# The low part of a pair's second weight tile by a VectorE subtraction in place of an accumulating DMA

## The chip, the cores and the metric

The kernel runs on one core of a Trainium2 chip. The time is device microseconds of one execution on that core. A kernel's time is the median of several runs. One execution more is taken by the hardware profiler, and all the rows shown below come from that one. The engines are named as in the profile: PE is TensorE's matmul, PEld its weight load, DVE is VectorE, ACT is ScalarE, POOL is GpSimd, SP is SyncE.

## The reference

One layer of a hybrid decoder runs over 520 columns (512 prompt positions and 8 sample positions). The part that matters here is the channel mixer at the end of the layer, with `wg`, `wu` of 1024 x 3072 and `wd` of 3072 x 1024, all float32:

```python
def conv_ffn(xn, prefix, wg, wu, cw, cb, wd):
    g_pre = xn @ wg
    ext = jnp.concatenate([prefix.astype(g_pre.dtype), g_pre], axis=1)
    h = jax.nn.gelu(causal_dwconv(ext, cw, cb)) * (xn @ wu)
    return h @ wd, ext[:, -(FFN_CONV - 1):]
...
    f, ffn_state = conv_ffn(rmsnorm(x, lp['norm2_g']), ffn_prefix, lp['ffn_wg'], lp['ffn_wu'],
                            lp['ffn_conv_w'], lp['ffn_conv_b'], lp['ffn_wd'])
    x = x + f
```

## The kernel before, in words

**Numbers in two parts.** A float32 weight tile is used as a sum of two float32r tiles: the high part `wh` is the tile rounded by an ACT copy, the low part `wl` is the tile minus its high part. The activations are split likewise. A product is three matmuls: high by high (`wh` with `X..h`), high weight by low activation (`wh` with `X..l`), and low weight by high activation (`wl` with `X..h`), in this order for each block of 128 rows (lines 202 to 207 and 256 to 258). A weight tile here is 128 x 1024 float32, 512 KB.

**Two ways to make a low part.** `Chunk.low` (line 120) makes it with a DVE subtraction of raw and high part (line 127). `low_by_dma` (line 97) makes it in two steps: ACT writes minus the high part into the low tile (line 99), and a DMA issued by POOL adds the weights from DRAM onto it (line 100). The DMA reads the weights from DRAM a second time, so it needs no raw tile. Ten chunks of the stage before the pairs go this second way too.

**The stages.** Up to about 472 us the mixers and their projections run, then comes the first part of the channel mixer with plain tiles. From 547.70 us to 900.69 us in the trace it runs in 18 **pairs** (`MP = 6`, lines 1055 to 1058): a pair is two column blocks of 128 of `wg` or of `wu`, nine pairs of `wg` and nine of `wu`, in turns. After the last pair come the last `wd` blocks and the final norm.

**One pair.** Its two raw tiles `raw[0]` and `raw[1]` are multiplied as 2 x 2 blocks by the half-size scheme with seven products. The weight operands are `h1` (`raw[1]` itself), `h0` (half of `raw[0]`), and two sums `h2`, `h3`, built by four DVE additions (lines 176 to 181). `run_pair` (line 244) emits PE's work as eleven steps by `SEQ_PAIR = (0, (0,0), 3, 2, (0,1), 1, 4, 5, (1,0), 6, (1,1))`: a number is one of the seven products, of 12 matmuls, and a bracket is half of one of two filler jobs, 12 matmuls of the `wd` product. So a pair is 132 matmuls. Product 0 takes the first half of `h1`, and the third matmul of the pair is the first that reads the low part of `h1`. Products 2 and 3 take the first halves of `h3` and `h2`, and product 6 takes `h0`.

**What sets the order.** Each engine works through its own list in the order in which the program emits it. After every step `run_later` emits the helper steps that are due. `Pair.steps` (line 189) gives their due times in steps, counted back from the start of the pair: the loads at -15, the sums at -8, -7 and -6, `high1` at -7, `low1` at -6, `high0` at -6, `low0` at -5, the high and low parts of `h2` and `h3` from -4 to -2, and the low part of `h3` at +1. So `high1` and `low1` of a pair are emitted about the middle of the pair before it. The filler's `wd` chunk is loaded at -9 steps and split at -3 (ACT) and -2 (DVE).

**Queues and buffers.** SP issues all weight loads in order. Raw tiles live in four buffers (`RAW = 4`), so a load waits until the last reader of an earlier tile is done. The list of SP shows the second load of a pair waiting for DVE and for ACT. High and low tiles have six buffers each (`HS`, `LS`). POOL issues the accumulating DMAs: `wl<-in_wg`, `wl<-in_wu` of line 100, and `x1d<-dn` of line 1004, which adds each filler's result (copied by ACT, line 1003) onto a DRAM buffer. The results of products leave PSUM through ACT copies (line 261) and DVE subtractions (lines 967 and 986).

Of the kernel before, what the change touches and what calls it, by code (L numbers as in the profile page):

```python
# [51 lines left out]
def trunk_kernel(ctx: ExitStack, tc: tile.TileContext, t: dict, o: dict):  # L52
    nc = tc.nc
    v, s, g, te = nc.vector, nc.scalar, nc.gpsimd, nc.tensor
# [26 lines left out]
    def f(x):  # L81
        return x.bitcast(F32)
# [14 lines left out]
    def low_by_dma(l, h, src):  # L97

        s.activation(l, f(h), AF.Copy, scale=-1.0)
        nc.gpsimd.dma_start(l, src, accum_op=ALU.add)  # L100
# [32 lines left out]
    class Pair:  # L133
# [27 lines left out]
            s.activation(self.new("h1", "wh"), self.raw[1], AF.Copy)  # L161

        def low1(self):
            low_by_dma(self.new("h1", "wl"), self.W["h1", "wh"], self.src[1])

        def high0(self):
            s.activation(self.new("h0", "wh"), self.raw[0][:, 512:], AF.Copy)
# [1041 lines left out]
```

## Time and profile before

| | us |
|---|---|
| median of 3 runs | 951.67 (946.41 to 952.67) |
| the profiled execution | 943.07 |
| its span, first to last instruction | 941.1 |
| PE busy in the span | 882.6 (94%) |
| DVE busy | 575.9 (61%) |
| ACT busy | 456.8 (49%) |
| POOL busy | 134.3 (14%) |

How to read it: busy is the time in which an engine had an instruction under way, and matmuls overlap, so a busy PE is not a PE at its peak. The rows of a timeline give start, duration, engine, line and operation, and in brackets how long the engine had been idle before and what it waited for. A wait is put down to the last of the things waited for. The granted clock (PEclk) is TensorE's, 1.00 being 2.4 GHz, and it has two levels here, 2.4 and 1.2 GHz.

### The profile page before, as it was taken

The page shows a single profiled execution, that of the slowest core. Times are in us where ns is not written, and L with a number is a line of the kernel's source. Part 1 is how long each engine was busy: PE and PEld are TensorE (multiplying, and loading weights), DVE is VectorE, ACT ScalarE, POOL GpSimd, SP SyncE. Part 2 cuts the span into 40 slices and gives each one's busy share as a digit, 9 for nine tenths or more (in the row PEclk, how much of TensorE's full clock was granted, in tenths as well). Part 3 has the DMA queues.
Part 4 walks back from the last instruction along what each step waited for, and adds up shares of the span by engine and source line. Part 5 has one row for each costly group of instructions (what it writes and reads, how often), then busy time and mean ns, then how long its engine had stood idle before and what let it go on. Part 6 is the DMA issues. An engine that isn't in the chain of part 4 may idle for free.

```text
span 941.1 us, 16904 instructions
## 1 busy us (share of the span) xinstructions
PE 882.6 (94%) x7142; PEld 874.7 (93%) x7142; DVE 575.9 (61%) x906; ACT 456.8 (49%) x651; POOL 134.3 (14%) x189
## 2 busy tenths in 40 slices
PE   9999999999999999999999997898887899889894
PEld 7999999999999999999999997888887899888894
DVE  5897987888844421555577756445555545754456
ACT  7555554773433332223477654445554455544540
POOL 1403311021000001000121411111111111111120
PEclk9999999999999999999999999899999899999997
DMA  9333233223232333324397686455666556765542
GB/s 303 125 103 112 68 102 101 68 77 103 69 112 83 96 113 127 122 90 136 135 223 161 136 186 149 113 112 136 130 150 140 120 113 144 167 138 114 113 125 92
DMA packets 38859, 117.84 MB, mean 125 GB/s; under 512 B 4456, under 2 KB 7656, under 8 KB 38760
## 3 DMA queue, kind: packets, MB, share of 16 engines
q1 hardware_dynamic: 25600, 83.21, 27.1%
q0 software_dynamic: 11808, 32.12, 20.2%
q10 hardware_dynamic: 1376, 1.44, 0.4%
q8 instruction: 56, 0.92, 0.4%
q14 instruction: 19, 0.16, 0.1%
HBM read 101.57 MB, written 15.57 MB: 124 GB/s over the span
## 4 chain that ended last, share of the span: by engine, by line
PE 62%; issue 29%; POOL 3%; DMA 2%; DVE 2%; ACT 1%; SPq 0%; POOLq 0%; DVEq 0%; ACTq 0%
PE pj L206 57%; POOL x1d L1004 2%; PE pa L257 1%; PE lru L206 1%; DMA wl<-in_wu 1%; DMA wl<-in_wg 1%; POOL wl L100 1%; DVE y L1034 1%; PE c L257 1%; DMA x<-in_x 0%; PE vm L745 0%; POOL fg L961 0%; PE po L206 0%; PE pf L257 0%; DVE bc L515 0%
## 5 line engine op out<-in xcount | busy, mean ns | idle before, releaser
L127 DVE TENSOR_TENSOR wl<-raw,wh 128x1024 fp32r<-128x1024 f32 (+1 forms) x108 | 126.5, 1176 | 42.4 <-ACT wh L118 42.4
L206 PE MATMUL pj<-xn_h,wh 128*128 128x260 f32 x704 | 141.9, 283 | 0.1
L206 PE MATMUL pj<-xn_l,wh 128*128 128x260 f32 x704 | 141.4, 282 | 0.0
L206 PE MATMUL pj<-xn_h,wl 128*128 128x260 f32 x704 | 140.8, 281 | 0.0
L118 ACT ACTIVATE wh<-raw 128x1024 fp32r<-128x1024 f32 (+1 forms) x118 | 117.6, 1005 | 4.9 <-DMA raw<-in_w_in 2.8
L206 PEld LDWEIGHTS pj<-xn_l,wh 128*128 128x128 f32 x704 | 108.6, 188 | 0.0
L206 PEld LDWEIGHTS pj<-xn_h,wh 128*128 128x128 f32 x704 | 108.1, 188 | 0.3 <-ACT r L533 0.3
L206 PEld LDWEIGHTS pj<-xn_h,wl 128*128 128x128 f32 x704 | 108.2, 188 | 0.0
L206 PE MATMUL pj<-h_l,wh 128*128 128x260 f32 x384 | 84.0, 299 | 0.0
L206 PE MATMUL pj<-h_h,wh 128*128 128x260 f32 x384 | 83.7, 298 | 0.0
L206 PE MATMUL pj<-h_h,wl 128*128 128x260 f32 x384 | 83.2, 297 | 0.0
L1004 POOL DMA_DIRECT2D x1d<-dn x40 | 34.9, 874 | 310.4 <-ACT dn L1003 300.2
L257 PE MATMUL pa<-X_h,wl 128*128 128x260 f32 x72 | 24.7, 343 | 43.6 <-DMA wl<-in_wu 24.3
L206 PEld LDWEIGHTS pj<-h_l,wh 128*128 128x128 f32 x384 | 65.3, 206 | 0.0
L206 PEld LDWEIGHTS pj<-h_h,wl 128*128 128x128 f32 x384 | 64.8, 204 | 0.0
L206 PEld LDWEIGHTS pj<-h_h,wh 128*128 128x128 f32 x384 | 64.4, 203 | 0.0
L257 PEld LDWEIGHTS pa<-X_h,wl 128*128 128x128 f32 x72 | 15.7, 218 | 47.1 <-DMA wl<-in_wu 26.2
L686 ACT ACTIVATE gt<-pj 128x520 f32<-128x520 f32 x24 | 14.5, 605 | 81.3 <-PE pj L206 81.2
L967 DVE TENSOR_TENSOR fg<-pf,m 128x260 f32<-128x260 f32 x9 | 3.9, 429 | 67.3 <-ACT dn L1003 36.9
L187 DVE TENSOR_TENSOR wl<-sum,wh 128x1024 fp32r<-128x1024 f32 x36 | 43.9, 1219 | 0.9 <-ACT wh L184 0.9
L261 ACT ACTIVATE m<-pa 128x260 f32<-128x260 f32 x36 | 14.0, 388 | 62.5 <-PE pa L257 62.4
L986 DVE TENSOR_TENSOR c<-pf,m 128x260 f32<-128x260 f32 x9 | 3.9, 429 | 57.1 <-ACT dn L1003 26.3
(480 smaller groups left out, 2430.1 us busy)
## 6 DMA issues: line engine op xcount, KB each, us to landing
raw<-in_w_in SPq DMA_DIRECT2D x50, 512.0 KB, 3.5
raw<-in_wg SPq DMA_DIRECT2D x24, 512.0 KB, 4.2
raw<-in_wu SPq DMA_DIRECT2D x24, 512.0 KB, 4.7
raw<-in_wd SPq DMA_DIRECT2D x24, 512.0 KB, 8.5
x1d<-dn POOLq DMA_DIRECT2D x40, 260.0 KB, 4.9
wl<-in_wu POOLq DMA_DIRECT2D x15, 512.0 KB, 9.4
wl<-in_wg POOLq DMA_DIRECT2D x13, 512.0 KB, 9.1
raw<-in_w_pb SPq DMA_DIRECT2D x8, 512.0 KB, 3.6
```

What stands on the lines that cost most here:

```text
L100: nc.gpsimd.dma_start(l, src, accum_op=ALU.add)
L118: s.activation(self.h[:, q], self.raw[:, q], AF.Copy)
L127: v.tensor_sub(self.l[:, q], self.raw[:, q], f(self.h[:, q]))
L187: v.tensor_sub(self.new(n, "wl"), self.s[n], f(self.W[n, "wh"]))
L206: te.matmul(ps[:, h, :TH], ww, xx[h] if isinstance(xx, list) else xx[:, h * TH:(h + 1) * TH], start=first and n == 0, stop=last and n == 2)
L257: te.matmul(bank[b], ww, xx, start=seen[b] + j + e == 0, stop=i >= (6, 1, 5)[b] and j == 3 and e == 2, skip_group_check=True)
L261: s.activation(kept["AFC"[b] + str(seen[b])], bank[b], AF.Copy)
L686: s.activation(two(y), acc(ps), AF.Sigmoid)
L967: v.tensor_sub(o_, a, b)
L986: v.tensor_sub(o_, a, b)
L1004: nc.gpsimd.dma_start(x1d[:, j, :], y, accum_op=ALU.add)
L1034: v.scalar_tensor_tensor(y[:, j - j0, :], x1[j][:, c], pc("gf", j), ps[:, 0, :TH], op0=ALU.mult, op1=ALU.mult)
```

## The change

`Pair.low1` calls the DVE subtraction in place of `low_by_dma`. The operands are the raw tile in SBUF and the high tile. Nothing else is edited: the due time stays at -6 steps.

```diff
         def low1(self):
-            low_by_dma(self.new("h1", "wl"), self.W["h1", "wh"], self.src[1])
+            v.tensor_sub(self.new("h1", "wl"), self.raw[1], f(self.W["h1", "wh"]))
```

In the lists of the engines it moves the following, once in each of the 18 pairs. On DVE, in the middle of a pair (here the first pair, of `wg`, while the next one is made ready): the sums L176 to L181 and `low0` (L170) belong to the next pair, L967 takes the running pair's product 1 (`pf`) and product 5 (`c`) out of PSUM, L187 makes the low part of `h2`. Before:

```order
L176 TENSOR_TENSOR sum<-raw 128x512
L177 TENSOR_TENSOR sum<-sum,raw 128x512
L179 TENSOR_TENSOR sum<-raw 128x512
L181 TENSOR_TENSOR sum<-sum,raw 128x512
L967 TENSOR_TENSOR fg_7023<-pf,m 128x260
L170 TENSOR_TENSOR wlq<-raw,whq 128x512
L967 TENSOR_TENSOR fg_7023<-c,m 128x260
```

And now:

```order
L176 TENSOR_TENSOR sum<-raw 128x512
L177 TENSOR_TENSOR sum<-sum,raw 128x512
L179 TENSOR_TENSOR sum<-raw 128x512
L181 TENSOR_TENSOR sum<-sum,raw 128x512
L164 TENSOR_TENSOR wl<-raw,wh 128x1024
L967 TENSOR_TENSOR fg_7019<-pf,m 128x260
L170 TENSOR_TENSOR wlq<-raw,whq 128x512
L967 TENSOR_TENSOR fg_7019<-c,m 128x260
```

The subtraction L164 stands new between the last sum of the next pair and the step that takes product 1 out of PSUM.

On ACT, in the same place (L161 is `high1` of the next pair, L167 its `high0`, L1003 copies the filler's result, L261 copies results of products). Before:

```order
L261 ACTIVATE m<-pa 128x260
L161 ACTIVATE wh<-raw 128x1024
L1003 ACTIVATE dn_6803<-pj 128x520
L99 ACTIVATE wl<-wh 128x1024
L167 ACTIVATE whq<-raw 128x512
L261 ACTIVATE k<-pa 128x260
```

And now:

```order
L261 ACTIVATE m<-pa 128x260
L161 ACTIVATE wh<-raw 128x1024
L1003 ACTIVATE dn_6801<-pj 128x520
L167 ACTIVATE whq<-raw 128x512
L261 ACTIVATE k<-pa 128x260
```

The negated copy L99 is gone, and what stood behind it moves up. On POOL the 18 issues of L100 go in the same way, and its x1d issues (L1004) then stand in a row. On PE the list of matmuls is the same in both. On SP the loads stand as before, but the second load of a pair, which waited for DVE and ACT, now waits for DVE alone.

## Rows read from the trace of the kernel before

**Rows 1.** Busy time by stretch; columns: stretch, its length, then busy us (and instructions) of PE, PEld, DVE, ACT and POOL, the granted clock, the share of the DMA engines and GB/s. The first stretch lies far ahead of the pairs, the second is all 18 pairs, then the first, the second, a later pair of `wg` and the `wu` pair after it.

```profile
236.30:471.70 235.40, 235.40 (x1970) 235.40 (x1969) 111.80 (x140) 80.69 (x103) 10.60 (x19) 1.00 0.34 109
547.70:900.69 352.99, 309.43 (x2380) 305.91 (x2379) 188.28 (x310) 179.15 (x275) 49.58 (x75) 0.94 0.61 133
547.70:563.53 15.83, 15.83 (x135) 15.83 (x134) 7.85 (x14) 9.88 (x15) 2.75 (x5) 1.00 0.73 134
563.53:582.18 18.65, 15.59 (x130) 15.39 (x129) 10.59 (x19) 9.85 (x16) 2.61 (x3) 1.00 0.61 133
704.69:724.93 20.24, 17.66 (x135) 17.45 (x134) 10.35 (x17) 10.40 (x16) 2.75 (x5) 0.92 0.59 124
724.93:745.50 20.57, 17.60 (x134) 17.39 (x133) 11.06 (x20) 9.86 (x16) 2.61 (x3) 0.92 0.59 128
```

**Rows 2.** The waits of PE from 560 to 930 us: engine, what waited, for what, us in total, times, longest.

```profile
PE pa L257 <- DMA wl<-in_wu: 24.3, 9, 3.8
PE pa L257 <- DMA wl<-in_wg: 19.3, 8, 2.7
PE n31p L452 <- DVE x2q L1019: 0.5, 1, 0.5
PE n30b L480 <- DVE n30d L459: 0.5, 1, 0.5
```

**Rows 3.** The timeline of PE at the start of a later pair of `wg`: its first three matmuls, and matmuls of fillers and products behind them.

```profile
704.69 0.29 PE L257 MATMUL pa<-X_h,wh 128*128 128x260 f32 x1
704.81 0.28 PE L257 MATMUL pa<-X_l,wh 128*128 128x260 f32 x1
707.67 0.39 PE L257 MATMUL pa<-X_h,wl 128*128 128x260 f32 x1 [2.58 <-DMA wl<-in_wg]
...
709.75 0.64 PE L206 MATMUL pj<-h_h,wl 128*128 128x260 f32 x2
...
714.85 0.40 PE L206 MATMUL pj<-h_h,wh 128*128 128x260 f32 x2
```

**Rows 4.** The timelines of ACT and POOL ahead of that pair: `high1`, the filler's copy, the negated copy, and the issue of its low part's DMA behind that of x1d.

```profile
695.10 1.05 ACT L161 ACTIVATE wh<-raw 128x1024 fp32r<-128x1024 f32 x1
696.23 0.61 ACT L1003 ACTIVATE dn<-pj 128x520 f32<-128x520 f32 x1
696.73 1.05 ACT L99 ACTIVATE wl<-wh 128x1024 fp32r<-128x1024 f32 x1
...
697.13 0.86 POOL L1004 DMA_DIRECT2D x1d<-dn  x1 [10.09 <-ACT dn L1003]
698.08 0.88 POOL L100 DMA_DIRECT2D wl<-in_wg  x1
```

**Rows 5.** The DMA issues from 560 to 900 us: what, queue, count, KB each, median us from issue to landing.

```profile
wl<-in_wg POOLq DMA_DIRECT2D x8, 512.0 KB, 9.5
wl<-in_wu POOLq DMA_DIRECT2D x8, 512.0 KB, 9.6
```

**Rows 6.** The DVE groups of all 18 pairs (547.7 to 900.7 us): line, operation, shapes, count, busy us, mean ns of one, idle time ahead of them and what ended it.

```profile
L127 DVE TENSOR_TENSOR wl<-raw,wh 128x1024 fp32r<-128x1024 f32 x19 | 23.2, 1220 | 7.0 <-ACT wh L118 7.0
...
L967 DVE TENSOR_TENSOR fg<-pf,m 128x260 f32<-128x260 f32 x9 | 3.9, 429 | 67.3 <-ACT dn L1003 36.9 <-PE pf L257 30.4
...
L986 DVE TENSOR_TENSOR c<-pf,m 128x260 f32<-128x260 f32 x9 | 3.9, 429 | 57.1 <-ACT dn L1003 26.3 <-PE pf L257 23.1 <-ACT wl L99 7.7
```

**Rows 7.** The first pair, which had no wait, and the head of the second: timeline of DVE.

```profile
549.69 0.69 DVE L181 TENSOR_TENSOR sum<-sum,raw 128x512 f32<-128x512 f32 x1
556.63 0.43 DVE L967 TENSOR_TENSOR fg<-pf,m 128x260 f32<-128x260 f32 x1 [6.25 <-PE pf L257]
557.19 0.69 DVE L170 TENSOR_TENSOR wlq<-raw,whq 128x512 fp32r<-128x512 f32 x1
559.41 0.43 DVE L967 TENSOR_TENSOR fg<-c,m 128x260 f32<-128x260 f32 x1 [1.52 <-PE c L257]
...
565.68 1.22 DVE L187 TENSOR_TENSOR wl<-sum,wh 128x1024 fp32r<-128x1024 f32 x1
566.82 0.69 DVE L176 TENSOR_TENSOR sum<-raw 128x512 f32<-128x512 f32 x1
...
568.75 0.68 DVE L181 TENSOR_TENSOR sum<-sum,raw 128x512 f32<-128x512 f32 x1
```

**Rows 8.** The same stretch on ACT, PE and SP: `high1` of the second pair and the copies around it; where the first pair's product 2 begins and where it first uses a low part; the two loads of the third pair (one row for both, the second issued at the end of the row's time), and a load of a `wd` chunk, which shows how long one issue takes.

```profile
553.94 1.05 ACT L161 ACTIVATE wh<-raw 128x1024 fp32r<-128x1024 f32 x1
...
565.80 0.64 ACT L855 ACTIVATE fc<-fc 128x520 f32<-128x520 f32 x1 [0.54 <-DVE fc L846]
568.49 0.39 ACT L261 ACTIVATE m<-pa 128x260 f32<-128x260 f32 x1 [2.05 <-PE pa L257]
...
552.02 0.28 PE L257 MATMUL pa<-X20h,wh 128*128 128x260 f32 x1
...
552.26 0.28 PE L257 MATMUL pa<-X20h,wl 128*128 128x260 f32 x1
...
545.16 10.18 SPq L153 DMA_DIRECT2D raw<-in_wg  x2
557.91 0.33 SPq L112 DMA_DIRECT2D raw<-in_wd  x1
```

**Rows 9.** Line 153 (the loads of the pairs' raw tiles): time from issue to landing, all 36.

```profile
DMA to landing us min/median/max: 3.4/4.3/6.8
```

## The prediction

> **What bounds the kernel now.** I read the busy time by stretch first, to see where PE, the engine with the most work, falls short of its own pace. Far ahead of the pairs it is busy without a gap at a granted clock of 1.00. The 18 pairs take 352.99 us, PE is busy for 309.43 of them, and the clock is 0.94 [rows 1]. The first pair is a measure of what a pair costs when nothing is late: 15.83 us, all busy, clock 1.00. The two later pairs shown take 20.24 and 20.57 us at 0.92 [rows 1]. So 18 undisturbed pairs would be 18 x 15.83 = 284.94 us, and the stage loses 352.99 - 284.94 = 68.05 us.
>
> The list of waits names the first part of the loss: PE waits 9 times for `wl<-in_wu` and 8 times for `wl<-in_wg`, 24.3 + 19.3 = 43.6 us, that is in 17 of 18 pairs, and the next entry is 0.5 us [rows 2]. The timeline shows the place: the first two matmuls of the pair run, the third, the first to read the low part of `h1`, comes 2.58 us late [rows 3]. The second part is the clock: behind the wait two filler matmuls take 0.64 us, later 0.40 [rows 3]. Over the stage it is 309.43 - 284.94 = 24.5 us of busy time too much, 1.44 us for each of 17 waits.
>
> Why it is late: `high1` starts at 695.10, the filler's copy and the negated copy follow, the x1d issue stands ahead on POOL, so that the DMA is issued at 698.08 [rows 4] and takes 9.5 us to land [rows 5]: 707.6, and PE goes on at 707.67 [rows 3].
>
> **The change part by part.**
>
> *Removed.* 18 negated copies on ACT (1.05 us each, [rows 4]), 18 issues on POOL (0.88 us) and 18 DMAs of 512 KB. ACT and POOL aren't waited for at that place, so their gain by itself is nothing. The DMA is what PE waits for, 43.6 us.
>
> *Added.* 18 subtractions on DVE. The same operation on the same shape is L127, 1.22 us [rows 6], 22 us in all. What hides them is DVE's idle time just behind them: before it takes product 1 out of PSUM, DVE idles 67.3 us in the nine `wg` pairs and 57.1 in the nine `wu` pairs [rows 6]. That idle time shrinks when the pairs do, so I look at the first pair, which already runs at the new pace: DVE idles 6.25 us up to 556.63 [rows 7]. The subtraction needs `high1`, which ends at 553.94 + 1.05 = 554.99 [rows 8]. It would run from 555.0 to 556.2 and leave DVE free 0.4 us before product 1 is there. Its result is wanted at 563.53 + 2 x 0.12 = 563.77, by the third matmul of the second pair ([rows 3] for the step of 0.12), so the low part is 7.5 us early instead of about 3 late. Were the cover gone, the price would be at most 18 x 1.22 = 22 us.
>
> *The new wait.* In DVE's list the subtraction waits for ACT's `high1`, and behind it stand the step that frees product 1's bank, `low0`, and the rest of the pair's chain. In the first pair `low0` starts at 557.19, after that step [rows 7], so with 0.4 us to spare nothing moves. The order behind product 5 (559.41 in [rows 7]) is the same as now.
>
> *What is late next.* The low part of `h3` is made last. In the first pair it ends at 565.68 + 1.22 = 566.90 [rows 7]. Product 2 reads its low part first at 552.26 - 547.70 = 4.56 us after a pair's start [rows 8], so an unstalled second pair wants it at 563.53 + 4.56 = 568.09: 1.2 us spare. On ACT the copy of product 0's result, which frees the bank for product 2, stands behind a gelu that starts at 565.80 [rows 8]. It would end at 565.80 + 0.64 + 0.39 = 566.83, against 563.53 + (552.02 - 547.70) = 567.85 for product 2's first matmul: 1.0 us spare. Both distances are set by product 5 of the pair before, not by the stall, so they hold in each pair.
>
> *The moved load.* The second raw tile is now also read by the subtraction, so the load that takes its place goes out about 1.2 us later. In the first pair it went at 545.16 + 10.18 - 0.33 = 555.0, the end of `high1` [rows 8]; now it is 556.2. The longest landing was 6.8 us [rows 9]: 563.0, and the first sum wants it at 566.82 [rows 7]. 3.8 us spare, so nothing. With the 18 x 512 KB of the accumulating DMAs gone, I expect loads no slower than now.
>
> *The clock.* The rows show 1.00 wherever PE runs without a gap, over 235 us, and in the first pair, and 0.92 where there is a wait [rows 1]. The second pair waited 3.06 us by its busy time (18.65 - 15.59) and kept 1.00 [rows 1], so not each wait costs clock, but none is lost without one. I take the whole 24.5 us as gained; the low end of this term is 0, if the clock falls for another reason. The Trainium skill, page "TensorE: Matmul & The Clock Gate", section "HAM oscillation — how this bites in real kernels", says that a loop of matmuls with a DMA wait in each round is throttled again at the waits and pays half rate each time. By that rule all of the 24.5 us goes and the profiled time is 875.0; with a clock that falls for other reasons it would be 899.5. The trace agrees with the rule in most pairs and not in the second.
>
> *The sum.* Against the profiled execution's 943.07 us (span 941.1): 43.6 for the waits and 24.5 for the clock, 0 for all else, is 68.05 (or 68.1 with the rounded terms): 943.07 - 68.05 = 875.0. This execution is 8.6 us below the median of the runs, 951.67, and below all three. If the 8.6 us lies in waits and clock, it goes too: 875.0. If it lies elsewhere, it stays: 883.6. No row decides this, so I take the middle, 879.
>
> **The rivals.**
>
> *A, part of the loss stays.* Either the clock term stays (943.07 - 43.6 = 899.5), or a small wait for `h3`'s low part or its bank takes the old wait's place. A wait of 1 us with the old clock loss in 17 pairs would be 17 x (1 + 1.44) = 41 us, so 916. For it: the spare time is only 1.0 to 1.2 us, in all pairs. Against it: the first pair ran at full pace with the same chain, and the added instruction doesn't stand in it. By the runs' median this is 890 to 925.
>
> *B, no change.* Something else is late at the same place and was hidden behind the DMA, so the edit moves the name of the wait and not its length: about 952. Against it: the operands of product 0 are the activations of before, the high part is ready at 695.10 + 1.05 = 696.15 [rows 4], and the `wd` parts have a filler's distance. Nothing in the rows holds PE at that place but the DMA.
>
> *C, slower: a loop through the raw tile.* The subtraction now holds `raw[1]`, the load of the next but one pair waits for it, the four sums wait for the load, and the next subtraction stands behind the sums in DVE's list. One turn of that loop is the landing time L, the sums from 566.82 to 569.43 (2.6 us, [rows 7]) and the subtraction's 1.22: L + 3.8 us a pair. It binds once L is over 12.0 us (15.83 - 3.8), and the kernel is slower than before once L + 3.8 is over the present mean, 352.99 / 18 = 19.6, so from L = 15.8 us. At L = 18 it would be 18 x 2.2 = 40 us more, 983 (992 by the median). Against it: these loads land in 3.4 to 6.8 us [rows 9], and the traffic falls. Even an accumulating DMA took only 9.5 [rows 5].
>
> **How the numbers follow.** Forecast 0.85, A 0.10, B 0.03, C 0.02. The predicted time is the forecast's, 879. Its own range: downward 875.0 less the spread of the three runs (952.67 - 946.41 = 6.3), 868.7; upward 883.6 and half a microsecond lost in each of 18 pairs (9.0), 892.6. So 868 to 893, which leaves 0.15 out and needs no part of A. A measurement of this kernel can tell about 1% from no change. Forecast and A are both over 1% faster: 0.95. Same 0.03, slower 0.02.
>
> **What would show it.** PE's waits in the pairs are no longer for a DMA of `wl`, and sum to a few us at most. Each pair takes about 15.8 us at a clock of 1.00, the stage about 285. DVE's new row L164 takes 1.22 us, starts right behind `high1`, and ends before DVE takes out product 1. ACT and POOL have 18 instructions fewer, and loads land within 7 us. I would be wrong if the pairs still show a granted clock near 0.92 without a wait (then A's clock), if PE waits at product 2 (A's other half), if the third matmul still waits, for DVE (B), or if the sums wait for the raw tile (C).

## The result, and the profile after

| | us |
|---|---|
| before, median of 4 runs | 949.04 (943.73 to 952.67) |
| after, median of 4 runs | 875.05 (874.69 to 875.17) |
| ratio, 95% interval | 0.9224 (0.9173 to 0.9275) |
| the profiled executions, before and after | 943.07 and 874.69 |
| their spans | 941.1 and 872.8 |

The kernel is 7.8% faster. The predicted time was 879 in a range of 868 to 893. The sum against the profiled execution gave 875.0.

The busy time by stretch, as in [rows 1], in the profile after: all 18 pairs, the first pair, and the second.

```profile
547.34:832.31 284.97, 284.97 (x2380) 284.97 (x2379) 207.64 (x327) 162.15 (x258) 34.54 (x58) 1.00 0.56 134
547.34:563.16 15.82, 15.82 (x134) 15.82 (x133) 8.97 (x15) 8.93 (x14) 1.87 (x4) 1.00 0.58 125
563.16:578.98 15.82, 15.82 (x134) 15.82 (x133) 12.21 (x21) 8.82 (x15) 1.73 (x2) 1.00 0.56 135
```

The stage takes 284.97 us, where the prediction had 18 x 15.83 = 284.94. PE is busy for all of it at a granted clock of 1.00. Before it took 352.99 us, so 68.0 us of the 68.4 us between the two profiled executions come from here.

The waits of PE, of the whole span after:

```profile
PE n31p L452 <- DVE x2q L1017: 3.3, 1, 3.3
PE warm L1084 <- DVE wz L1081: 1.5, 1, 1.5
PE n31b L480 <- POOL n31d L459: 1.4, 1, 1.4
PE n31p L452 <- DVE x2q L1019: 0.5, 1, 0.5
PE n30b L480 <- DVE n30d L459: 0.5, 1, 0.5
PE n31b L480 <- DVE n31d L459: 0.3, 1, 0.3
PE pj L206 <- ACT wh L118: 0.3, 1, 0.3
```

The two DMA entries of [rows 2], 43.6 us, are gone, and nothing has come in their place within the pairs: what is left belongs to the start and to the final norm.

The DVE groups of the pairs after, to be read against [rows 6]:

```profile
L164 DVE TENSOR_TENSOR wl<-raw,wh 128x1024 fp32r<-128x1024 f32 x17 | 20.8, 1226 | 31.8 <-ACT wh L161 31.8
L967 DVE TENSOR_TENSOR fg<-pf,m 128x260 f32<-128x260 f32 x9 | 3.9, 429 | 2.5 <-PE pf L257 2.5
L986 DVE TENSOR_TENSOR c<-pf,m 128x260 f32<-128x260 f32 x9 | 3.9, 429 | 3.9 <-PE pf L257 3.9
```

The idle time ahead of product 1's removal, 124 us before, now is 31.8 us ahead of the subtraction, which waits for `high1`, and 2.5 + 3.9 us behind it. The rest is gone because the pairs are shorter.

The first pair after and the head of the second, timeline of DVE, and rows of ACT, PE and SP:

```profile
554.66 1.23 DVE L164 TENSOR_TENSOR wl<-raw,wh 128x1024 fp32r<-128x1024 f32 x1 [4.65 <-ACT wh L161]
556.24 0.43 DVE L967 TENSOR_TENSOR fg<-pf,m 128x260 f32<-128x260 f32 x1 [0.35 <-PE pf L257]
...
565.33 1.22 DVE L187 TENSOR_TENSOR wl<-sum,wh 128x1024 fp32r<-128x1024 f32 x1
566.46 0.69 DVE L176 TENSOR_TENSOR sum<-raw 128x512 f32<-128x512 f32 x1
...
565.99 0.37 ACT L261 ACTIVATE m<-pa 128x260 f32<-128x260 f32 x1
...
567.48 0.28 PE L257 MATMUL pa<-X20h,wh 128*128 128x260 f32 x1
...
567.72 0.28 PE L257 MATMUL pa<-X20h,wl 128*128 128x260 f32 x1
...
555.92 0.33 SPq L153 DMA_DIRECT2D raw<-in_wg  x1
```

This is [rows 7, 8] shifted by about 0.36 us with the subtraction put in: it leaves DVE free 0.35 us before product 1 is there, the low part of `h3` is ready at 566.55, 1.17 us before product 2 reads it, the copy that frees product 2's bank ends at 566.36, 1.12 us before product 2's first matmul, and the load goes out as the subtraction ends. These loads land in 3.3 to 6.0 us, median 3.9, against [rows 9].

### The profile page after: what moved, and what is told of

Same layout as the page of the kernel before. It is cut to its first block, busy times and chain, and to the rows that moved or that the text cites. A ratio compares the mean times of both kernels' runs of the same rounds, so it can differ in the third digit from the quotient of the medians.

```text
span 872.8 us, 16856 instructions
## 1 busy us (share of the span) xinstructions
PE 858.1 (98%) x7142; PEld 853.9 (98%) x7142; DVE 596.1 (68%) x924; ACT 438.9 (50%) x633; POOL 119.4 (14%) x171
## 3 DMA queue, kind: packets, MB, share of 16 engines
q10 hardware_dynamic: 1376, 1.44, 0.5%
## 4 chain that ended last, share of the span: by engine, by line
PE 97%; DVE 2%; ACT 0%; DMA 0%; issue 0%; DVEq 0%; ACTq 0%
PE pj L206 73%; PE pa L257 12%; PE c L257 6%; PE pf L257 3%; PE lru L206 1%; DVE y L1034 1%; PE vm L745 0%; DMA par<-in_par 0%; PE po L206 0%; DVE bc L515 0%; PE vt L738 0%; ACT L533 0%; DVE n L468 0%; PE n31p L452 0%; PE n30p L452 0%
## 5 line engine op out<-in xcount | busy, mean ns | idle before, releaser
L206 PE MATMUL pj<-h_l,wh 128*128 128x260 f32 x384 | 78.6, 282 | 0.0
L206 PE MATMUL pj<-h_h,wh 128*128 128x260 f32 x384 | 78.6, 283 | 0.0
L1004 POOL DMA_DIRECT2D x1d<-dn x40 | 34.9, 874 | 266.0 <-ACT dn L1003 259.6
L206 PEld LDWEIGHTS pj<-h_l,wh 128*128 128x128 f32 x384 | 59.7, 188 | 0.0
L206 PEld LDWEIGHTS pj<-h_h,wl 128*128 128x128 f32 x384 | 59.7, 188 | 0.0
L206 PEld LDWEIGHTS pj<-h_h,wh 128*128 128x128 f32 x384 | 59.6, 188 | 0.0
L187 DVE TENSOR_TENSOR wl<-sum,wh 128x1024 fp32r<-128x1024 f32 x36 | 43.9, 1220 | 0.9 <-ACT wh L184 0.9
L164 DVE TENSOR_TENSOR wl<-raw,wh 128x1024 fp32r<-128x1024 f32 x18 | 22.1, 1226 | 31.8 <-ACT wh L161 31.8
L184 ACT ACTIVATE wh<-sum 128x1024 fp32r<-128x1024 f32 x36 | 37.8, 1050 | 0.8 <-DVE sum L179 0.8
L844 DVE SCALAR_TENSOR_TENSOR fc<-fg,par,fc 128x512 f32<-128x512 f32 x48 | 36.0, 750 | 1.1 <-ACT fc L840 0.3
L951 ACT ACTIVATE h_h<-fc 128x520 fp32r<-128x520 f32 x24 | 15.4, 640 | 25.4 <-DVE fc L983 11.1
L1003 ACT ACTIVATE dn<-pj 128x520 f32<-128x520 f32 x40 | 23.9, 598 | 6.6 <-PE pj L206 5.0
```

The source lines that it names most:

```text
L164: v.tensor_sub(self.new("h1", "wl"), self.raw[1], f(self.W["h1", "wh"]))
L184: s.activation(self.new(n, "wh"), self.s[n], AF.Copy)
L187: v.tensor_sub(self.new(n, "wl"), self.s[n], f(self.W[n, "wh"]))
L206: te.matmul(ps[:, h, :TH], ww, xx[h] if isinstance(xx, list) else xx[:, h * TH:(h + 1) * TH], start=first and n == 0, stop=last and n == 2)
L844: v.scalar_tensor_tensor(y[:, :SEQ], ext[:, r:r + SEQ], pc("fcw", r * MF + m), y[:, :SEQ], op0=ALU.mult, op1=ALU.add)
L951: after(0.25, lambda: s.activation(h, y, AF.Copy))
```

## The experiments

The question was what the 68 us had been paid for. Theory 1: for lateness alone, a part that PE wants about 2.6 us before it is there, plus the clock that the wait costs. Theory 2: for the accumulating DMA itself, its second reading of 9.4 MB, its POOL issues and ACT copies. Theory 3 was rival A of the prediction: that the clock has other reasons. Two more questions were how much room there is on DVE, and what bounds the kernel now.

**The DMA kept, but issued earlier** (e1 and e10, from the kernel before):

```diff
-            return ((-15, self.load), (-8, lambda: self.sums(0)), (-7, lambda: self.sums(1)), (-7, self.high1),
-                    (-6, lambda: self.sums(2)), (-6, self.low1), (-6, self.high0), (-5, self.low0),
+            return ((-15, self.load), (-8, lambda: self.sums(0)), (-7, lambda: self.sums(1)), (-10, self.high1),
+                    (-6, lambda: self.sums(2)), (-10, self.low1), (-6, self.high0), (-5, self.low0),
```

and with -8 for both in e10 (one step sooner than before for `high1`, two for `low1`).

> The accumulating DMA stays, but the high part of h1 and its negated copy are emitted 10 steps ahead of the pair instead of 7 and 6, right behind the copy of product 0's result. Theory (the wait is lateness alone, issue plus 9.5 us of landing): the copy ends about 5.2 us into the pair before, the DMA is issued at about 5.2 to 6.1 us and lands at about 14.7 to 15.6, against 16.1 when PE wants it; the 43.6 us of waits and the 24.5 us of clock go nearly all, 875 to 890 us. Rival (the DMAs cost by their 9.4 MB of traffic, their POOL issues or ACT copies, wherever they stand): the time stays over 910 us.

> The kernel before with the high part of h1 and its negated copy 8 steps ahead of the pair (before: 7 and 6; the early DMA: 10). Theory (lateness alone): the DMA is issued about 7.0 us into the pair before, 2 us earlier than in the kernel before, and PE wants it at 16.1 us; with a landing of 7.4 to 9.5 us it is late by 0 to 0.5 us: 875 to 888 us. Rival (the DMA costs its full wait at any place but the earliest): over 915 us.

Measured: 874.98 us for e1, ratio 0.9248 (0.9208 to 0.9287), and 875.55 us for e10, ratio 0.9252 (0.9225 to 0.9278). PE has no wait for `wl` in either. The timeline of POOL in e1, where the second pair starts about 563.3:

```profile
565.34 0.86 POOL L1004 DMA_DIRECT2D x1d<-dn  x1 [8.57 <-ACT dn L1003]
568.83 0.88 POOL L100 DMA_DIRECT2D wl<-in_wg  x1 [2.63 <-ACT k L261]
571.58 0.86 POOL L1004 DMA_DIRECT2D x1d<-dn  x1 [1.87 <-ACT dn L1003]
```

and the issues of e1 from 547 to 832 us, as in [rows 5]:

```profile
wl<-in_wu POOLq DMA_DIRECT2D x9, 512.0 KB, 5.7
wl<-in_wg POOLq DMA_DIRECT2D x8, 512.0 KB, 7.4
```

All 18 DMAs, negated copies and issues are still there, and the time is that of the kernel after. So the DMA costs nothing by itself here. Theory 2 falls, and two steps of due time are worth as much as the whole change.

The earlier issue did not act alone. The issue of the second pair's DMA before, where the first pair starts at 547.70, then in e10, where it starts at 547.89, and the issues of e10 from 547 to 832 us:

```profile
556.93 0.88 POOL L100 DMA_DIRECT2D wl<-in_wu  x1
...
555.13 0.89 POOL L100 DMA_DIRECT2D wl<-in_wu  x1 [5.22 <-ACT m L261]
...
wl<-in_wu POOLq DMA_DIRECT2D x9, 512.0 KB, 6.4
wl<-in_wg POOLq DMA_DIRECT2D x8, 512.0 KB, 6.7
```

The DMA goes out 2.0 us sooner in the pair, and it also lands about 3 us faster than the 9.5 of [rows 5]. So what PE waited for is the moment of landing, and the due time moved both terms of it, the issue and the landing time.

**The low part made late by DVE** (e2, from the kernel after):

```diff
+        def touch1(self):
+            l = self.W["h1", "wl"]
+            v.tensor_scalar(l, f(l), 1.0, None, op0=ALU.mult)
...
-                    (1, lambda: self.low("h3")))
+                    (0, self.touch1), (1, lambda: self.low("h3")))
```

> The kernel after, with one operation more: at the pair's start DVE multiplies the low part of h1 by 1.0 in place, so that it is ready as late as the DMA made it, but by DVE. Theory (lateness is all, whoever causes it, and the clock falls with the wait): DVE comes to it about 2 us into the pair, in both kinds of pair, it takes 0.6 to 1.2 us, PE waits 2.3 to 3.0 us in 17 pairs, 39 to 51 us, and 15 to 25 us of clock come with it: 930 to 950 us. Rival 1 (the clock falls for another reason than the wait): 915 to 925 us with a granted clock that stays at 0.99. Rival 2 (the DMA itself is the cost): under 885 us.

Measured: 922.06 us, ratio 0.9744 (0.9701 to 0.9786), 47.0 us over the kernel after. That is 8 us under the range expected: PE waits 30.9 us in 17 pairs, since in `wg` pairs DVE comes to the operation 0.7 us into the pair (583.12, the pair starting at 582.39), not 2 as I had reckoned, and the wait is 1.07 us, not 2.3 or more. By its time alone e2 lies in the range of rival 1, but that rival wanted a clock that stays at 0.99. The stage of the 18 pairs in e2, with the granted clock at 0.96:

```profile
547.98:879.12 331.14, 300.23 (x2379) 296.71 (x2378) 216.93 (x344) 163.18 (x258) 35.13 (x58) 0.96 0.47 115
```

PE is busy for 300.23 us of it, 15.3 more than in the kernel after. About 0.25 us for each of the 17 waits, 4.3 us, is lost at full clock too (the same in e5, where the clock stayed up); the other 11 us are the clock. The timeline of PE of e2, a wait that lost no clock:

```profile
566.70 0.39 PE L261 MATMUL pa<-X_h,wl 128*128 128x260 f32 x1 [2.50 <-DVE wl L168]
568.01 0.40 PE L210 MATMUL pj<-h_h,wh 128*128 128x260 f32 x2
```

and one of the same length that did:

```profile
602.43 0.39 PE L261 MATMUL pa<-X_h,wl 128*128 128x260 f32 x1 [2.48 <-DVE wl L168]
604.00 0.64 PE L210 MATMUL pj<-h_h,wh 128*128 128x260 f32 x2
...
606.17 0.64 PE L210 MATMUL pj<-h_h,wl 128*128 128x260 f32 x2
```

With no DMA in it the same kind of wait brings the same kind of loss: both parts belong to lateness, whoever is late. Theory 3 falls: waits put back bring the low clock back, though not at each wait.

**Only the `wu` pairs changed** (e7, from the kernel before; `sub` is true for `wu`, and the lines that hand it to the pair are left out here):

```diff
         def low1(self):
-            low_by_dma(self.new("h1", "wl"), self.W["h1", "wh"], self.src[1])
+            if self.sub:
+                v.tensor_sub(self.new("h1", "wl"), self.raw[1], f(self.W["h1", "wh"]))
+            else:
+                low_by_dma(self.new("h1", "wl"), self.W["h1", "wh"], self.src[1])
```

> The subtraction only in the nine wu pairs; the nine wg pairs keep the accumulating DMA. Theory (each pair's gain is its own wait and clock): what is left are the eight waits for wl of wg, 19.3 us, and 8 x 1.44 = 11.5 us of clock, so 875 + 31 = 906 us, between 900 and 912. Rival (what is removed in one pair comes back in the next): 925 to 945 us.

Measured: 906.29 us, ratio 0.9579 (0.9537 to 0.9621). The waits of PE:

```profile
PE pa L260 <- DMA wl<-in_wg: 21.8, 8, 4.0
```

21.8 us of waits and 9.4 us more make the 31.2 us over the kernel after. The gain is a sum over pairs: next to nothing removed in one pair comes back in the next, though the eight waits that are left come to 21.8 us where they were 19.3 before [rows 2]. The clock fell at four of the eight.

**Room on DVE** (e3: the new subtraction twice; e4 and e5: the low part of `h3` two and three times; all from the kernel after):

```diff
-            v.tensor_sub(self.new("h1", "wl"), self.raw[1], f(self.W["h1", "wh"]))
+            l = self.new("h1", "wl")
+            for _ in range(2):
+                v.tensor_sub(l, self.raw[1], f(self.W["h1", "wh"]))
```

```diff
-            v.tensor_sub(self.new(n, "wl"), self.s[n], f(self.W[n, "wh"]))
+            l = self.new(n, "wl")
+            for _ in range(2 if n == "h3" else 1):
+                v.tensor_sub(l, self.s[n], f(self.W[n, "wh"]))
```

In e5 there is a 3 in place of the 2.

> The kernel after with the new subtraction done twice in a row, 18 more DVE instructions of 1.22 us. Theory (it lies in idle time of DVE, and a delay of product 1's removal from PSUM reaches nobody): DVE takes product 1 out 0.8 us later, PE waits for nothing, 873 to 877 us. Rival (DVE has become the bound of the pair): 18 x 0.8 to 18 x 1.2 us more, 889 to 897 us.

> The kernel after with the low part of h3, the last part made for a pair, subtracted twice in a row: it is ready 1.13 us later. Theory (its spare time is 1.2 us where a wg pair goes before and 1.7 us where a wu pair does): PE waits for nothing or a few tenths in nine pairs, 873 to 879 us. Rival (there is no such spare time, DVE is at its limit): 17 x 1.1 us more, 890 us or over.

> The same with three subtractions: 2.27 us later. Theory: PE waits at product 2 for DVE, about 1.1 us in nine pairs and 0.6 us in eight, 14 to 15 us, and 0.2 to 0.5 us of slower start or clock each: 888 to 900 us. Rival (the low part of h3 is not what is late next): 873 to 879 us, as with two.

Measured: e3 874.64 us, ratio 0.9245 (0.9198 to 0.9293); e4 876.93, ratio 0.923 (0.918 to 0.9281); e5 895.53, ratio 0.9428 (0.9376 to 0.9479). In e3 the removal of product 1 is put off and PE doesn't notice, timeline of DVE:

```profile
555.06 2.48 DVE L166 TENSOR_TENSOR wl<-raw,wh 128x1024 fp32r<-128x1024 f32 x2 [4.62 <-ACT wh L161]
557.46 0.42 DVE L969 TENSOR_TENSOR fg<-pf,m 128x260 f32<-128x260 f32 x1
```

In e5 the next late part shows, in the waits of PE:

```profile
PE pa L259 <- DVE wl L189: 16.4, 17, 1.3
```

One more subtraction (1.13 us) ahead of `h3`'s low part uses up its spare time: in e4 a `wu` pair, which has a `wg` pair before it, takes about 16.06 us instead of 15.82, with no wait long enough to be listed, which makes up e4's 1.9 us. The second is paid: 1.24 us where a `wg` pair goes before and 0.67 us where a `wu` pair does. Rival A of the prediction names the right part, and what kept it away is 1.17 us in the one kind of boundary and about 1.7 us in the other.

**The other accumulating DMAs** (e6, from the kernel after): the ten plain chunks ahead of the pairs get the subtraction too.

```diff
-            job([(Chunk(src[i], KD, timed=True, by_dma=post is u2_post or m >= 2), 0, plain if m >= MN else (lambda k: xg2[k]))],
+            job([(Chunk(src[i], KD, timed=True, by_dma=False), 0, plain if m >= MN else (lambda k: xg2[k]))],
```

> The kernel after, and the ten plain chunks ahead of the pairs that take an accumulating DMA get the subtraction too, 10 x 1.22 us more on DVE, 10 DMAs, negated copies and POOL issues fewer. Theory (only a part that PE waits for is worth anything, and PE waits for none of these): 873 to 877 us. Rival (removing the DMAs is worth something by itself, as traffic or as ACT and POOL time): 865 to 872 us. Other rival (DVE is short of time in that stage, 9 tenths busy in places): 880 to 890 us.

Measured: 874.61 us, ratio 0.9206 (0.9146 to 0.9266). No difference that can be told from 875.05. The same edit, at a place where nobody waits for the part, is worth nothing.

**Earlier loads** (e8, from the kernel before):

```diff
-NA, RAW, HS, LS, LOADS, HLEAD, LLEAD = 51, 4, 6, 6, 3, 3, 2
+NA, RAW, HS, LS, LOADS, HLEAD, LLEAD = 49, 5, 6, 6, 3, 3, 2
```

> The kernel before with five raw buffers instead of four and 49 instead of 51 activation buffers, so that the weight loads go out earlier. Question: is the landing of 9.5 us the DMA's own, or is it the loads beside it? Theory (the loads that are issued at the same time stretch it, since the early DMA landed in 5.7 and 7.4 us): landing 6 to 8 us, PE's waits shrink from 43.6 to 5 to 25 us, 885 to 925 us. Rival (the landing at that place is the DMA's own): 9 to 10 us, and the time stays at 940 to 950 us.

Measured: 950.73 us, ratio 1.0014 (0.9975 to 1.0053), no change. The issues from 560 to 900 us:

```profile
raw<-in_wd SPq DMA_DIRECT2D x19, 512.0 KB, 3.6
...
raw<-in_wu SPq DMA_DIRECT2D x15, 512.0 KB, 6.3
raw<-in_wg SPq DMA_DIRECT2D x14, 512.0 KB, 7.3
...
wl<-in_wg POOLq DMA_DIRECT2D x8, 512.0 KB, 10.0
wl<-in_wu POOLq DMA_DIRECT2D x8, 512.0 KB, 9.8
```

My expectation failed, and the experiment doesn't settle its question. The load of `wd` left the place (3.6 us instead of 8.7), but with five buffers the loads of the next pair came to stand beside the accumulating DMA in its stead. In e1, with one or two such loads beside it, it landed in 5.7 to 7.4 us. That the neighbours stretch it fits all these kernels. No run changed the neighbours alone, but ahead of the pairs the trace before has two of these DMAs, issued at 507.30 and 523.97, beside which a single weight load was under way, which landed about 2 us after their issue:

```profile
wl<-in_wg POOLq DMA_DIRECT2D x1, 512.0 KB, 6.5
...
wl<-in_wu POOLq DMA_DIRECT2D x1, 512.0 KB, 5.6
```

They speak for the neighbours and against the rival, though they come from another stage.

**More pairs** (e9, from the kernel after):

```diff
-MN, MP = 4, 6
-XSTEP = (0.4, 0.4)
+MN, MP = 4, 4
+XSTEP = (0.2, 0.2)
```

> The kernel after with pairs from block 4 on instead of 6 (two pairs more, 20 in all) and the operands for them made twice as fast (a step of 0.2 instead of 0.4). What is tested: whether the kernel after is now bound by the number of matmuls alone. Theory: a pair has 84 product matmuls where two plain blocks have 96, so two pairs save 24 matmuls of 0.12 us, 2.9 us: 871 to 873 us. Rival (the operands or the first pair's parts come too late at that place): 876 to 890 us, with waits of PE ahead of the first pair.

Measured: 882.89 us, ratio 0.9324 (0.9296 to 0.9352), 0.9% over the kernel after, though it has fewer matmuls. The waits of PE, the first and fifth:

```profile
PE pa L257 <- DVE wl L164: 5.5, 1, 5.5
...
PE pj L206 <- DVE wl L127: 0.7, 1, 0.7
```

Busy time by stretch, around that place:

```profile
505.00:530.00 25.00, 18.64 (x120) 17.95 (x119) 23.81 (x36) 10.66 (x17) 6.68 (x5) 0.80 0.20 64
```

The rival was right: at the start of the first pair DVE is busy for 23.81 of 25 us with the operands, and there the very subtraction of this change comes 5.5 us late, with a granted clock of 0.80 in that stretch. Its price of nothing holds where DVE idles, not everywhere. I have no version that beats the kernel after by more than can be measured.

## Why the prediction was right

- *What bounds.* Right. The stage lost 68.05 us against 18 undisturbed pairs, and 68.0 us came back.
- *The waits, 43.6 us.* Right, and e1 and e10 say what they were: the due time, with the copy, the queue and the landing behind it, not the DMA as such. The 9.5 us of landing was not fixed either: in e10 it was 6.4 to 6.7.
- *The clock, 24.5 us.* Right in its sum, but my 1.44 us for each wait is a mean over two cases. Taking the distance between two waits less 15.83 us and less the second wait, 12 of the 16 that can be so measured in the trace before give 1.65 to 1.83 us and 4 give 0.25 to 0.30. The 0.25 us is there after each wait, e2's and e5's too, where the clock stayed at 1.00; the other 1.5 us is the clock. So of the 24.5 us about 17 x 0.25 = 4.3 is the price of the waits themselves and about 20 the clock. The term's low end was then 4.3 and not 0, and the time with a clock that falls for other reasons about 895, not 899.5.
- *The subtraction hidden.* Right to 0.05 us: 0.35 us of idle time behind it, where I had reckoned 0.4. e3 shows that even this room wasn't needed.
- *What is late next.* Right: `h3`'s low part, with 1.17 us to spare (1.2 reckoned), and the bank of product 2 with 1.12 (1.0 reckoned). That both hold in each pair was not right: behind a `wu` pair `h3`'s low part has about 1.7 us. e4 and e5 lie on both sides of the 1.17.
- *The moved load.* Right: issued at the subtraction's end, no wait, and loads no slower.
- *The sum.* 875.0 against 874.69 for the profiled execution and 875.05 for the median. Mis-sized was the step from the profiled execution to the median: I took the middle between keeping and losing the 8.6 us, and it all went. The runs of before spread from 941.57 to 956.65 over the sessions, those of after from 874.69 to 875.17. That the spread was in the waits and the clock fits this, and the mean granted clock, 0.961 in the slowest execution and 0.969 in the fastest, but only one execution of before has a trace, so it is not shown. Taking the middle was a guess, and it cost 4 us.
- *The rule of the Trainium skill* ("TensorE: Matmul & The Clock Gate", section "HAM oscillation — how this bites in real kernels"). I took it too widely. The loop of that section waits longer for its DMA than it computes, and in the section's table a loop that computes far longer than it waits keeps the full clock. Here a pair computes 15.8 us and waits 1.8 to 3.8, so by the section the clock should have stayed up. The runs differ from it: 12 of the 16 waits above lost clock. They differ from my reading of it, "each time", as well: of eight waits of 2.5 us in e2 six lost clock, and of eight of 1.07 us none did. That the term came out all the same rests on the rows, which showed no loss without a wait.

## What to carry to other kernels

Before a wait for a transfer is charged to the transfer, look when it was issued: here a DMA that seemed to cost 7% cost nothing once it was asked for two steps sooner. Price the removal of a wait from a stretch of the same trace that has no wait, not from the wait alone, since what came behind it, most of it the clock, was over a third of the gain. An operation added to an idle engine is free only in the stretch in which that engine idles, so look for the next part to be late, and how early it is now.

## What the runs showed that I had not expected

- At waits of the same length the clock is lost or not lost. In e2 eight of the waits that can be so measured lasted 2.48 to 2.50 us; after six of them the pair took 1.78 to 1.84 us too long, after two 0.25 us. Before, a wait of 3.06 us lost none and one of 1.88 lost it (1.81 us). The length of the wait alone doesn't tell which it will be. Waits of up to 1.3 us (17 in e5, 8 of 1.07 us in e2) lost none. The loss isn't always one size either: in e7 a wait of 3.75 us cost 2.6 us beyond its idle time.
- The clock doesn't fall at a fixed time after a wait. In the trace before, from 586.27 to 750.11 us, it fell nine times, each 20.48 us after the last, while the waits ended 19.65 to 21.41 us apart. So the fall came anywhere from 0.3 us before PE went on to 1.5 us after. Here it came while PE still waited, up to 607.04 (columns as in [rows 1], the granted clock goes from 1.00 to 0.50):

```profile
606.25:606.75 0.50, 0.00 (x0) 0.00 (x0) 0.50 (x1) 0.00 (x0) 0.00 (x0) 1.00 1.21 161
606.75:608.75 2.00, 1.71 (x8) 1.71 (x9) 1.96 (x4) 0.00 (x0) 0.00 (x0) 0.50 0.73 124
```

When a wait comes, and not only how long it is, may decide whether it loses clock. No run moved a wait by itself, so this stays open.
- Each wait of PE costs about 0.25 us beyond the idle time that the profile shows.
- An accumulating DMA of 512 KB landed in 5.7 to 10.0 us (medians of e1 and e8), in kernels that differ in when it goes out and in what is under way beside it.
